# Folded feed-forward units: weight preparation in a written order, modulation dots spread singly

## The chip, the cores and the metric

The kernel runs on one core of a Trainium2 chip. The metric is the device time of one execution in microseconds (us); of several runs the median is taken. Engines are named as in the profile: PE is TensorE (matrix products; PEld are its weight loads), DVE is VectorE, ACT is ScalarE, POOL is GpSimd, SP is SyncE, which issues nearly all DMA transfers.

## The reference

A two-layer model on 256 latent and 256 context tokens of width 1024, in float32. Each layer is a half feed-forward block, a mixer (attention in layer 0, an mLSTM scan in layer 1) and a second half feed-forward block. The change concerns the second feed-forward block of layer 0 and the first of layer 1:

```python
def half_ffn(h, shift, scale, gate, w_in, w_out, g, b):
    xm = modulate(h, shift, scale)              # h * (1 + scale) + shift
    a, u = jnp.split(xm @ w_in, 2, axis=-1)     # 1024 -> 2 x 2816
    y = (jax.nn.silu(a) * u) @ w_out            # 2816 -> 1024
    return post_norm(h, 0.5 * gate * y, g, b)   # layer norm of ALPHA * h + delta
mod_lat = jnp.split((jax.nn.silu(c) @ ada_w[i] + ada_b[i])[:, None, :], N_MOD, axis=-1)
mod_ctx = jnp.split((jax.nn.silu(c_ctx) @ ada_w[i] + ada_b[i])[None, None, :], N_MOD, axis=-1)
```

The shifts, scales and gates are products of a vector with ada_w. They are needed by the blocks that come later.

## The kernel before

**Splitting.** Every float32 operand of a large product is split into a high part, a cast to a reduced format on ScalarE (the copy in split, L212), and a low part, what is left of it, a subtraction on VectorE (L217). A product (mm3) is three matmuls: high by high (L229), high by low (L232), low by high (L233). Activations stand transposed: xh and xl hold 8 blocks d of 128 features by 512 tokens, of which 0 to 255 are latent (LAT) and 256 to 511 context (CTX).

**Weights.** A chunk is 128 x 1024 floats, 512 KB, loaded by raw (L197) from SP's queue into one of 4 buffers and split into one of 7 pairs of buffers (pair, WB = 7). A buffer is used again when its last reader is done.

**A feed-forward block (ffn).** The 22 hidden units of 128 (pairs a and u) are worked in parts. FOLD = {1: ((7, 7, 8), 2), 2: ((6, 8, 8), 1)}: block 1 (second of layer 0) has parts of 7, 7 and 8 units, of which the parts from number 2 on are folded; block 2 (first of layer 1) has 6, 8 and 8, folded from part 1 on. For each part, first unit_in makes g = silu(a) * u for each unit (ffn_g: silu L539 on ScalarE, product L540 on VectorE, split), then unit_out adds the part's share to each of the 8 output blocks d (sum_out, L587 on VectorE). The first 4 units (LEAD) of a block are run on the latent half while the normalization of the context half still goes on, and then on the context half. The last 6 output blocks of the last part (FOLDTAIL) are run by halves, with the next normalization stepped in between (its first product is L398, which needs the sum of L375).

**Folded units** use seven products of quarter size (Strassen's form in Winograd's order) in the place of eight. The inputs' sums are made once, by fold_x (called in the output loop of the part before, at d = 0 and d = 2): sums of high and low (L662), their differences (L666 to L669) and splits, four of them, the last overwriting the context half of xh and xl. The weights' sums are made for each unit by fold_w: two chunks are loaded, r0 is split, half of r1 is split, four sums are made in place (L695 to L698), and r0 and r1 are split once more; that is one cast of 512 columns and three of 1024 on ScalarE, one low part of 512, three of 1024 and four sums on VectorE. In folded, begin(j) calls fold_w(j) and then yields between the seven products (L724); the loop puts the last three products of the unit ahead among the first four of this one. Accumulators are reused: o2 is a copy of o0 after the first product (L735), o0 is copied out to u after the second (L738) and after the fourth (L744), and the sixth product adds to o0 again. VectorE adds to u (L748, L754) and closes the unit (L756).

**Order.** A scheduler in the compiler orders each engine's instructions by program order, by data ready in its own model of time, and by free buffers. Instructions that are passed to pin stay behind the instruction of their engine that stands before them in the program. Before the change, the products of folded units and the dots are pinned; the preparation of weights and the evacuations (L735 to L756) are not.

**Modulation (ada).** A row block of ada_w (512 KB) is loaded by ada_load (L302) into one of two buffers, and ada_dot (L308, on VectorE, pinned) multiplies it with silu(c) or silu(c_ctx) and sums: two dots per row in block 1 (40 rows), one in block 2 (32 rows). FOLDPOP says how many rows are loaded and dotted after which unit or output block: a row's load is issued right ahead of its dots.

## Time and profile before

| | |
|---|---|
| median of 3 runs | 1685.17 us (1683.67 to 1687.54) |
| profiled execution | 1678.48 us, span 1676.4 us |
| granted PE clock over the span | 0.995 |
| busy over the span | PE 97%, PEld 87%, DVE 83%, ACT 43%, POOL 6% |
| block 1 / block 2 of the change, in the span | about 590 to 960 us / 956 to 1330 us |
| the three folded sections (L724) | 819 to 905, 1052 to 1132, 1175 to 1259 us |

Matmuls are pipelined: one that takes 0.28 us in the record starts 0.11 us after the one before it, so loss on PE is read from starts, or from its waits. A row of the waits is "engine, line that waited <- engine, line that ended the wait: us in total, times, longest". A row of the groups is "line, engine, operation, operands, shapes, count | busy us, mean ns of one | idle us of the engine just before them <- what ended it". A row of the timeline is "start us, us, engine, line, operation, shapes, count [idle before <- what ended it]". A row of the windows is "from:to length, PE, PEld, DVE, ACT, POOL busy us (instructions), granted clock, DMA share, GB/s".

### The profile page before, as it was taken

How to read it: one execution, taken by the hardware profiler on the slowest of the kernel's cores; microseconds unless marked ns; L12 is line 12 of the kernel's file. 1: busy time of each engine (PE TensorE's matmuls, PEld its weight loads, DVE VectorE, ACT ScalarE, POOL GpSimd, SP SyncE). 2: the span in 40 equal slices, each digit the busy share in tenths (PEclk: the TensorE clock that was granted, in tenths of full speed). 3: DMA queues.
4: the chain of work that ended last, by engine and by line, in shares of the span. 5: the costliest groups of instructions: out<-in, count | busy, mean ns of one | idle time of the engine just before them, and what ended most of it. 6: DMA issues, size and time to landing. Idle time of an engine off the chain costs nothing. (4 is left out here: it accounts for less than half of the span.)

```text
span 1676.4 us, 26966 instructions
## 1 busy us (share of the span) xinstructions
PE 1617.8 (97%) x10320; PEld 1459.1 (87%) x10320; DVE 1387.7 (83%) x2971; ACT 726.5 (43%) x1286; POOL 93.5 (6%) x114
## 2 busy tenths in 40 slices
PE   7999999999889999999999999999999999999997
PEld 6888888899888897888899998998999888999986
DVE  5799977649988898978987898888888967997686
ACT  4622222314566353223354352552552646566541
POOL 0000000002331100000000100000001002120000
PEclk9999999999999999999999999999999999999999
DMA  9667765522201337765235253346343332337552
GB/s 352 205 216 240 237 212 190 180 69 86 64 1 56 121 108 237 224 198 176 63 101 164 78 195 119 101 152 207 124 160 114 108 126 76 116 124 252 178 176 75
DMA packets 71921, 250.63 MB, mean 150 GB/s; under 512 B 7920, under 2 KB 10480, under 8 KB 71792
## 3 DMA queue, kind: packets, MB, share of 16 engines
q1 hardware_dynamic: 71072, 248.15, 45.7%
q8 instruction: 81, 1.33, 0.3%
q10 hardware_dynamic: 720, 0.76, 0.1%
q14 instruction: 48, 0.39, 0.1%
HBM read 247.83 MB, written 1.05 MB: 148 GB/s over the span
## 5 line engine op out<-in xcount | busy, mean ns | idle before, releaser
L229 PE MATMUL t<-t,t 128*128 128x256 f32 (+2 forms) x2164 | 710.3, 330 | 12.3 <-ACT t L212 9.2
L232 PE MATMUL t<-t,t 128*128 128x256 f32 (+2 forms) x2164 | 710.7, 329 | 2.0 <-DVE t L493 1.1
L233 PE MATMUL t<-t,t 128*128 128x256 f32 (+2 forms) x2164 | 707.5, 328 | 3.1 <-DVE t L217 3.1
L212 ACT CAST t<-t 128x1024 fp32r<-128x1024 f32 (+2 forms) x523 | 442.2, 869 | 498.6 <-PE t L233 189.6
L217 DVE TENSOR_TENSOR t<-t,t 128x256 fp32r<-128x256 f32 (+2 forms) x871 | 547.8, 664 | 99.7 <-ACT t L212 96.5
L229 PEld LDWEIGHTS t<-t,t 128*128 128x128 f32 x2164 | 406.6, 189 | 52.8 <-ACT t L212 11.9
L232 PEld LDWEIGHTS t<-t,t 128*128 128x128 f32 x2164 | 408.7, 189 | 41.0 <-DVE t L493 2.0
L233 PEld LDWEIGHTS t<-t,t 128*128 128x128 f32 x2164 | 407.6, 189 | 41.2 <-DVE t L217 3.7
L308 DVE SCALAR_TENSOR_TENSOR t<-t,t 128x1024 bf16<-128x1024 f32 x224 | 263.2, 1220 | 11.9 <-DMA t<-in_ada_w 11.6
L724 PE MATMUL t<-t,t 128*128 128x256 f32 x2016 | 235.0, 278 | 8.2 <-ACT t L744 3.7
L724 PEld LDWEIGHTS t<-t,t 128*128 128x128 f32 x2016 | 233.1, 188 | 10.6 <-ACT t L744 4.5
L539 ACT ACTIVATE t<-t 128x256 f32<-128x256 f32 (+1 forms) x69 | 33.2, 487 | 131.3 <-PE t L233 130.1
L435 POOL TENSOR_TENSOR t<-t,t 128x256 f32<-128x256 f32 x30 | 23.3, 777 | 1149.4 <-ACT t L425 1147.9
L540 DVE TENSOR_TENSOR t<-t,t 128x256 f32<-128x256 f32 (+1 forms) x69 | 37.4, 549 | 52.9 <-PE t L233 40.3
L587 DVE SCALAR_TENSOR_TENSOR t<-t,t,t 128x256 f32<-128x256 f32 x128 | 57.3, 477 | 28.3 <-PE t L233 28.2
L900 PE MATMUL t<-t,t 128*128 128x256 f32 (+1 forms) x256 | 79.4, 312 | 0.0
L902 PE MATMUL t<-t,t 128*128 128x256 f32 (+1 forms) x256 | 78.8, 310 | 0.0
L901 PE MATMUL t<-t,t 128*128 128x256 f32 (+1 forms) x256 | 78.6, 309 | 0.0
L1339 PE MATMUL t<-t,t 128*128 128x512 f32 (+1 forms) x248 | 55.9, 378 | 10.5 <-ACT t L292 5.0
L1339 PEld LDWEIGHTS t<-t,t 128*128 128x128 f32 x248 | 47.1, 223 | 18.8 <-ACT t L292 5.0
L842 PE MATMUL t<-t,t 128*128 128x512 f32 x264 | 60.0, 389 | 0.0
L425 ACT ACTIVATE t<-t 128x256 f32<-128x256 f32 x72 | 26.1, 413 | 75.1 <-DVE t L418 75.1
(185 smaller groups left out, 1337.6 us busy)
## 6 DMA issues: line engine op xcount, KB each, us to landing
t<-in_ffn_in SPq DMA_DIRECT2D x168, 512.0 KB, 4.3
t<-in_ada_w SPq DMA_DIRECT2D x139, 512.0 KB, 4.0
t<-in_ffn_out SPq DMA_DIRECT2D x66, 512.0 KB, 4.5
t<-in_ffn_last SPq DMA_DIRECT2D x22, 512.0 KB, 3.6
t<-in_att_in SPq DMA_DIRECT2D x12, 512.0 KB, 3.5
t<-in_att_out SPq DMA_DIRECT2D x8, 512.0 KB, 4.0
t<-in_ml_qk SPq DMA_DIRECT2D x8, 512.0 KB, 3.5
t<-in_ml_v SPq DMA_DIRECT2D x8, 512.0 KB, 4.5
```

Source lines behind the costliest of these rows:

```text
L212: self.behind(self.nc.scalar.copy(h, x))
L217: self.behind(self.nc.vector.tensor_tensor(out=ls, in0=xs, in1=hs.bitcast(F32), op=ALU.subtract))
L229: ins = mm(out, wh, xh, start=first, stop=False)
L232: mm(out, wh, xl, start=False, stop=False)
L233: mm(out, wl, xh, start=False, stop=last)
L308: ins = nc.vector.scalar_tensor_tensor(self.tmp().bitcast(BF16), r, 1.0, self.cb[:, v, :], ALU.mult, ALU.mult, accum_out=to)
L724: self.pin(nc.tensor.matmul(o, p, q, start=first and k == i == 0, stop=k == half - 1 and i == 2, skip_group_check=True))
L842: pin(nc.tensor.matmul(ys[tt][i], gs[g], ws[k][w][:, i * 512 : (i + 1) * 512], start=k == 0 and g == w == 0, stop=k == NF - 1 and g == 1,))
L900: mm(o, self.xh[:, k, c], wh, start=k == 0, stop=False)
L901: mm(o, self.xh[:, k, c], wl, start=False, stop=False)
L902: mm(o, self.xl[:, k, c], wh, start=False, stop=k == ND - 1)
L1339: mm = lambda *k, **kw: pin(nc.tensor.matmul(*k, **kw))
```

## The change

- **Weights of folded units.** fold_w no longer loads; fold_load does, two units ahead. The preparation is five steps (first: half split for the last product and two sums; second: split for products one and three; sums: two sums; third and fourth: the two splits of sums). In folded, the steps for unit j + 1 stand between the products of unit j and the last three of unit j - 1, and every instruction there is pinned on its engine, the evacuations too. The order of the products on PE is the one that it was.
- **First folded unit of a section.** Its steps stand before the last output blocks of the part before (load before d = 4, first before 5, second and sums before 6, third and fourth before 7).
- **Output weights after a section.** The first two chunks of w_out are loaded at the last unit but one and split in the last unit's steps.
- **Sums of the inputs.** fold_x stands before the last two unit_in of the part ahead, without the fourth sum; that one, which overwrites xh and xl, is fold_x3 in the output loop at d = 0 and 1 and makes two of its sums again.
- **Modulation.** FOLDPOP gives way to DOTS: (n, points) spreads n calls over points. A unit_in has 4 points (after k = 1, 3, 5, 7), a unit_out 2. A call is one dot; the call of a row's first dot issues the next row's load ahead of it. The first call of a block only loads.

The diff, cut to its core ("unit" in folded is begin without fold_w, with every evacuation pinned and one more yield after the first product):

```diff
-FOLDPOP = {
-    1: {
-        "in": {0: 1, 1: 1, 2: 2, 3: 2, 4: 3, 5: 3, 6: 3} | {j: 2 for j in range(7, 14)},
-        "out": {0: (1, 1, 1, 1, 1, 1, 1, 1), 1: (0, 0, 0, 0, 1, 1, 1, 0)},
-        "tail": {},
-    },
-    2: {
-        "in": {0: 2, 1: 2, 2: 2, 3: 2, 4: 2, 5: 2},
-        "out": {0: (0, 0, 0, 0, 0, 0, 0, 0), 1: (2, 2, 2, 2, 2, 2, 1, 1), 2: (2, 2)},
-        "tail": {(0, 0): 1, (0, 1): 1},
-    },
+DOTS = {
+    1: {"lead": (12, 16), "in0": (14, 12), "out0": (17, 16), "in1": (38, 28)},
+    2: {"lead": (14, 16), "out0": (5, 16), "out1": (14, 12)},
 }
-FOLDX = {0: 0, 2: 1}
...
+        self.raws = {}
+
+    def load(self, c):
+        self.raws[c] = self.b.raw(self.chunks[c])
 
     def __call__(self, i, w=P):
         c, o = divmod(i * P, 1024)
         if c not in self.all:
-            self.all[c] = self.b.chunk(self.chunks[c], self.sh(c))
+            self.all[c] = self.b.chunk(self.chunks[c], self.sh(c), self.raws.get(c))
...
+            seen = {}
+
+            def tick(name):
+                seen[name] = seen.get(name, -1) + 1
+                side.get(("tick", name), lambda m: None)(seen[name])
+
+            def unit_in(j, w, g, steps={}, name=None):
                 n = g[1] - g[0]
                 pa, pu = self.mm(), self.mm()
                 for k in range(ND):
                     for part, o in ((0, pa), (1, pu)):
                         self.mm3(o[:, :n], w(k * 2 + part), self.x(k, g), k == 0, k == ND - 1)
                     self.steps(steps.get((j, k), ""))
+                    if name and k % 2:
+                        tick(name)
                 self.ffn_g(j, pa, pu, g)
 
             def unit_out(hf, d, w, g, steps={}):
                 y = self.mm()
-                part_out(hf, d, w, g, y, range(parts[hf]), steps)
+                n = parts[hf]
+                for js in (range(n // 2), range(n // 2, n)):
+                    part_out(hf, d, w, g, y, js, steps)
+                    if g == allg:
+                        tick(f"out{hf}")
...
+                            unit_in(j, ws[j], g, LEADSTEP if g == LAT else {}, "lead" if g == CTX else None)
+                    for j in first:
                         call("in", j)
                     js = js[LEAD:]
                 folded = None
+                w = (Keep if fold else Stream)(self, [w_out[ends[hf] - parts[hf] + i] for i in range(parts[hf])])
                 if hf >= folds:
                     self.fine = False
-                    folded = self.folded(js, w_in)
+                    folded = self.folded(js, w_in, w, ready)
                     js = []
                 for j in js:
-                    unit_in(j, stream(j), allg)
+                    if fold and hf == folds - 1 and j >= ends[hf] - 2:
+                        self.fold_x(2 * (j + 2 - ends[hf]))
+                    unit_in(j, stream(j), allg, name=f"in{hf}")
...
+                nj = ends[hf]
+                prep = {}
+                if folds <= hf + 1 < len(parts):
+                    self.open = None
+                    rs = []
+                    w22, it = self.fold_w(rs)
+                    go = lambda: next(it)()
+                    prep = {
+                        ND - 4: (lambda: rs.extend(self.fold_load(nj, w_in)),),
+                        ND - 3: (go,),
+                        ND - 2: (go, go),
+                        ND - 1: (go, go),
+                    }
                 for d in range(begun, body):
+                    for f in prep.get(d, ()):
+                        f()
                     unit_out(hf, d, w, allg)
                     call("out", hf, d)
-                    if fold and hf == folds - 1 and d in FOLDX:
-                        self.fold_x(2 * FOLDX[d])
+                    if fold and hf == folds - 1 and d < 2:
+                        self.fold_x3(2 * d)
+                if prep:
+                    ready = w22, self.fold_load(nj + 1, w_in)
                 if body < ND:
                     w = Keep(self, w.chunks, SH, w)
                     self.fine = True
                     for g in groups:
                         for d in range(body, ND):
                             unit_out(hf, d, w, g, tailstep)
-                            call("tail", int(g == CTX), d - body)
...
+    def fold_whole(self, d, g):
+        f = self.tmp().rearrange("p (d f) -> p d f", d=2)
+        h, l = (x[:, d : d + 2, g[0] : g[1]].bitcast(F32) for x in (self.xh, self.xl))
+        self.nc.vector.tensor_tensor(out=f, in0=h, in1=l, op=ALU.add)
+        return f
+
     def fold_x(self, k):
 
-        V, S = self.nc.vector, self.nc.scalar
+        V, S, whole = self.nc.vector, self.nc.scalar, self.fold_whole
         if k == 0:
             self.th, self.tl = (self.t([P, 3, ND // 2, TL], F32R, pool=self.gp) for _ in range(2))
-
-        def whole(d, g):
-            f = self.tmp().rearrange("p (d f) -> p d f", d=2)
-            h, l = (x[:, d : d + 2, g[0] : g[1]].bitcast(F32) for x in (self.xh, self.xl))
-            V.tensor_tensor(out=f, in0=h, in1=l, op=ALU.add)
-            return f
-
-        f11, f12, f21, f22 = whole(k, LAT), whole(k, CTX), whole(ND // 2 + k, LAT), whole(ND // 2 + k, CTX)
-        V.tensor_tensor(out=f11, in0=f11, in1=f12, op=ALU.subtract)
-        V.tensor_tensor(out=f12, in0=f22, in1=f12, op=ALU.subtract)
-        V.tensor_tensor(out=f22, in0=f22, in1=f11, op=ALU.add)
-        V.tensor_tensor(out=f21, in0=f22, in1=f21, op=ALU.subtract)
         ks = slice(k, k + 2)
         to = [[x[:, i, ks, :] for x in (self.th, self.tl)] for i in range(3)]
-        to3 = [x[:, ks, CTX[0] : CTX[1]] for x in (self.xh, self.xl)]
+        f11, f12 = whole(k, LAT), whole(k, CTX)
+        V.tensor_tensor(out=f11, in0=f11, in1=f12, op=ALU.subtract)
         self.split(f11, *to[0])
+        f22 = whole(ND // 2 + k, CTX)
+        V.tensor_tensor(out=f22, in0=f22, in1=f11, op=ALU.add)
         h, l = to[1]
         S.activation(h, f22, AF.Copy, scale=-1.0)
         V.scalar_tensor_tensor(l, f22, -1.0, h.bitcast(F32), ALU.mult, ALU.subtract)
-        self.split(f12, *to3)
+        f21 = whole(ND // 2 + k, LAT)
+        V.tensor_tensor(out=f21, in0=f22, in1=f21, op=ALU.subtract)
         self.split(f21, *to[2])
 
-    def fold_w(self, j, w_in):
-
-        V = self.nc.vector
-        r0, r1 = (self.raw(w_in[2 * j + i]) for i in range(2))
+    def fold_x3(self, k):
+
+        f12, f22 = self.fold_whole(k, CTX), self.fold_whole(ND // 2 + k, CTX)
+        self.nc.vector.tensor_tensor(out=f12, in0=f22, in1=f12, op=ALU.subtract)
+        self.split(f12, *(x[:, k : k + 2, CTX[0] : CTX[1]] for x in (self.xh, self.xl)))
+
+    def fold_load(self, j, w_in):
...
+    def fold_w(self, rs):
+
+        V, S, pin = self.nc.vector, self.nc.scalar, self.pin
         a = slice(0, 512), slice(512, 1024)
-        ps = [self.pair(sh=SH)]
-        self.split(r0, *ps[0])
-        if self.open is None:
-            p, self.open = self.pair(sh=SH), 1
-            self.halves, c = p, a[0]
-        else:
-            p, self.open = self.halves, None
-            c = a[1]
-        w22 = [x[:, c] for x in p]
-        self.split(r1[:, a[0]], *w22)
-        V.tensor_tensor(out=r1[:, a[0]], in0=r1[:, a[0]], in1=r1[:, a[1]], op=ALU.add)
-        V.tensor_tensor(out=r1[:, a[1]], in0=r1[:, a[1]], in1=r0[:, a[0]], op=ALU.add)
-        V.tensor_tensor(out=r0[:, a[0]], in0=r0[:, a[0]], in1=r1[:, a[0]], op=ALU.add)
-        V.tensor_tensor(out=r0[:, a[1]], in0=r0[:, a[1]], in1=r0[:, a[0]], op=ALU.add)
-        for r in (r0, r1):
+        cut = lambda p, i: [x[:, a[i]] for x in p]
+        high = lambda p, r: pin(S.copy(p[0], r))
+        low = lambda p, r: pin(V.tensor_tensor(out=p[1], in0=r, in1=p[0].bitcast(F32), op=ALU.subtract))
+        add = lambda o, p, q: pin(V.tensor_tensor(out=o, in0=p, in1=q, op=ALU.add))
+        w = {}
+
+        def first():
+            r0, r1 = rs
+            if self.open is None:
+                self.open = self.pair(sh=SH)
+                c = 0
+            else:
+                c = 1
+            w["22"] = cut(self.open, c)
+            if c:
+                self.open = None
+            high(w["22"], r1[:, a[0]])
+            low(w["22"], r1[:, a[0]])
+            add(r1[:, a[0]], r1[:, a[0]], r1[:, a[1]])
+            add(r1[:, a[1]], r1[:, a[1]], r0[:, a[0]])
+
+        def second():
+            r0, r1 = rs
             p = self.pair(sh=SH)
-            self.split(r, *p)
-            ps.append(p)
-        cut = lambda p, i: [x[:, a[i]] for x in p]
-        return {"11": cut(ps[0], 0), "12": cut(ps[0], 1), "22": w22,
-                "s2": cut(ps[1], 0), "s4": cut(ps[1], 1), "s1": cut(ps[2], 0), "s3": cut(ps[2], 1)}
-
-    def folded(self, js, w_in):
-
-        nc, V, S = self.nc, self.nc.vector, self.nc.scalar
+            w["11"], w["12"] = cut(p, 0), cut(p, 1)
+            high(p, r0)
+            low(p, r0)
+
+        def sums():
+            r0, r1 = rs
+            add(r0[:, a[0]], r0[:, a[0]], r1[:, a[0]])
+            add(r0[:, a[1]], r0[:, a[1]], r0[:, a[0]])
+
+        def third():
+            r0, r1 = rs
+            p = self.pair(sh=SH)
+            w["s1"], w["s3"] = cut(p, 0), cut(p, 1)
+            high(p, r1)
+            low(p, r1)
+
+        def fourth():
+            r0, r1 = rs
+            p = self.pair(sh=SH)
+            w["s2"], w["s4"] = cut(p, 0), cut(p, 1)
+            high(p, r0)
+            low(p, r0)
+
+        return w, iter((first, second, sums, third, fourth))
...
         before = iter(())
-        for j in js:
-            now = begin(j)
-            next(now)
-            for _ in range(2):
-                next(before, None)
-            for _ in range(2):
-                next(now)
-            next(before, None)
-            next(now)
+        step = lambda g: next(g, None)
+        w, rs = ready
+        nop = lambda: None
+        for i, j in enumerate(js):
+            now = unit(j, w)
+            if i + 1 < len(js):
+                w, prep = self.fold_w(rs)
+            else:
+                prep = iter((nop, lambda: w_out(0), nop, nop, lambda: w_out(len(js))))
+            if i + 2 < len(js):
+                rs = self.fold_load(js[i + 2], w_in)
+            elif i + 2 == len(js):
+                for c in range(2):
+                    w_out.load(c)
+            step(now)
+            next(prep)()
+            step(now)
+            step(before)
+            next(prep)()
+            next(prep)()
+            step(before)
+            next(prep)()
+            step(now)
+            next(prep)()
+            step(now)
+            step(before)
+            step(now)
             before = now
...
+            state = [None, None, 0]
+
+            def dot():
+                cur, nxt, v = state
+                if cur is None:
+                    state[0] = ada[0], b.ada_load(*ada.pop(0)[:2])
+                    return
+                if nxt is None and ada:
+                    state[1] = ada[0], b.ada_load(*ada.pop(0)[:2])
+                (layer, dt, vecs), r = cur
+                b.ada_dot(r, layer, dt, vecs[v])
+                state[2] = v + 1
+                if v + 1 == len(vecs):
+                    state[:] = [state[1], None, 0]
+
+            def tick(m, n, points):
+                for _ in range((m + 1) * n // points - m * n // points):
+                    dot()
+
+            for k, (n, points) in fold.items():
+                s["tick", k] = lambda m, n=n, points=points: tick(m, n, points)
```

50 lines of the change are left out of this document (20 added, 30 removed).

## The prediction

> **What bounds the kernel now.** The page comes first. The profiled execution took 1678.48 us: a span of 1676.4 and 2.1 around it. The median of the three timed runs is 1685.17, 6.7 above; I work the sum against the profiled execution and carry the difference over to the median.
>
> ```profile
> span 1676.4 us, 26966 instructions
> ...
> PE 1617.8 (97%) x10320; PEld 1459.1 (87%) x10320; DVE 1387.7 (83%) x2971; ACT 726.5 (43%) x1286; POOL 93.5 (6%) x114
> ...
> t<-in_ada_w SPq DMA_DIRECT2D x139, 512.0 KB, 4.0
> ```
>
> TensorE is the bound and the change leaves its products and their order alone, so all it can win is idle TensorE time in the two feed-forward blocks that it touches (640 to 1345 us). Hence the next view: TensorE's waits, window by window: 660 to 680; 815 to 905 (first folded section); 1050 to 1130 (second); 1130 to 1180 (start of the third); 1265 to 1345. Columns: total us, times, longest.
>
> ```profile
> PE t L229 <- ACT t L212: 2.2, 1, 2.2
> PE t L232 <- DVE t L217: 0.6, 1, 0.6
> ...
> PE t L724 <- ACT t L212: 2.6, 1, 2.6
> PE t L724 <- ACT t L744: 1.7, 2, 1.5
> PE t L724 <- DVE t L217: 0.8, 1, 0.8
> ...
> PE t L724 <- ACT t L744: 2.0, 2, 1.3
> PE t L724 <- ACT t L735: 0.4, 1, 0.4
> ...
> PE t L724 <- ACT t L735: 0.7, 1, 0.7
> ...
> PE t L398 <- DVE t L375: 1.7, 2, 1.0
> ```
>
> That is the whole purse: some 12 us. Waits that remain elsewhere in these blocks belong to the normalization, which is not changed.
>
> The second loss shows in no wait. Folded matmuls of 256 columns run at two paces; the rows of L724 in 1057 to 1088 us and in 1181 to 1231 us:
>
> ```profile
> L724 PE MATMUL t<-t,t 128*128 128x256 f32 x276 | 31.4, 276 | 0.0
> ...
> L724 PE MATMUL t<-t,t 128*128 128x256 f32 x426 | 50.3, 281 | 0.0
> ```
>
> Taking one duration off the end, (31.4 - 0.28) / 275 is 113 ns from start to start, (50.3 - 0.28) / 425 is 118 ns. A unit has 7 products of 12 matmuls, so 84 take 9.5 us or 9.9 us. The second and third sections both open with a wait for the copy at L735; after it the second runs at 113 ns and later has waits, the third at 118 ns and has none.
>
> **The change, part by part.**
>
> *Dots ahead of the first output product (window 660 to 680).* TensorE first, then DVE:
>
> ```profile
> 667.12 0.39 PE L233 MATMUL t<-t,t 128*128 128x512 f32 x1
> 669.69 0.50 PE L229 MATMUL t<-t,t 128*128 128x512 f32 x1 [2.18 <-ACT t L212]
> 671.11 0.39 PE L233 MATMUL t<-t,t 128*128 128x512 f32 x1
> ...
> 666.01 1.22 DVE L308 SCALAR_TENSOR_TENSOR t<-t,t 128x1024 bf16<-128x1024 f32 x1 [0.98 <-DMA t<-in_ada_w]
> 668.30 0.68 DVE L540 TENSOR_TENSOR t<-t,t 128x512 f32<-128x512 f32 x1
> ```
>
> From 667.12 to 671.11 are 3.99 us for three matmuls that take 0.23 each: 3.3 us lost. The cause is on DVE: the product of the gates (L540) of unit 6 waits behind dots (L308), and one of these waits 0.98 us for its row. The change takes 4 dots out of the stretch before it (18 after units 4 to 6 become 14), spreads them singly and asks for each row a dot earlier. The gates' product may then be up to about 2.6 us late: 18 matmuls (4.1 us) come ahead of the one that needs it, less product and cast. A dot takes 1.15 (from 666.01 to 668.30 are two); four are 4.6 us, more than the 3.3. I take -3.3 (ends: 0 and -3.3).
>
> *Weights of the first folded unit.* They move from the section's start to the output products before it.
>
> ```profile
> 818.92 1.58 PE L724 MATMUL t<-t,t 128*128 128x256 f32 x12
> 823.11 0.50 PE L724 MATMUL t<-t,t 128*128 128x256 f32 x2 [2.61 <-ACT t L212]
> 824.37 0.86 PE L724 MATMUL t<-t,t 128*128 128x256 f32 x5 [0.76 <-DVE t L217]
> ```
>
> From 818.92 to 824.37 are 5.45 us for 14 matmuls worth 1.65: 3.8 lost, waiting for the third and fourth casts of the unit and their low part. What stays is the copy of the first product (L735), which the second product of a first unit has to wait for in every section: 0.7 in the third. So -3.0 (ends: 0 and -3.1). Sections two and three have only that wait at their start: 0.
>
> *The fixed order in the loop.* Same instructions, now pinned on ScalarE and VectorE. What matters is the ring that closes once per unit. Rows of 1181 to 1238 us, VectorE and then ScalarE; then three low parts in a row, and one sum two units apart:
>
> ```profile
> L217 DVE TENSOR_TENSOR t<-t,t 128x1024 fp32r<-128x1024 f32 x16 | 19.3, 1219 | 3.9 <-ACT t L212 3.9
> L217 DVE TENSOR_TENSOR t<-t,t 128x512 fp32r<-128x512 f32 x11 | 7.5, 688 | 2.4 <-ACT t L212 2.4
> L698 DVE TENSOR_TENSOR t<-t 128x512 f32<-128x512 f32 x6 | 4.1, 689 | 0.1
> L756 DVE SCALAR_TENSOR_TENSOR t<-t,t 128x512 f32<-128x512 f32 x5 | 3.4, 689 | 0.7 <-DVE t L754 0.5
> L748 DVE TENSOR_TENSOR t<-t,t 128x256 f32<-128x256 f32 x6 | 2.5, 420 | 1.1 <-PE t L724 1.1
> ...
> L212 ACT CAST t<-t 128x512 fp32r<-128x512 f32 x11 | 6.7, 619 | 7.6 <-DMA t<-in_ffn_in 3.4 <-PE t L724 2.5 <-DVE t L756 1.7
> ...
> 1058.11 3.50 DVE L217 TENSOR_TENSOR t<-t,t 128x1024 fp32r<-128x1024 f32 x3 [1.69 <-ACT t L212]
> ...
> 1196.68 0.69 DVE L697 TENSOR_TENSOR t<-t,t 128x512 f32<-128x512 f32 x1
> 1216.56 0.69 DVE L697 TENSOR_TENSOR t<-t,t 128x512 f32<-128x512 f32 x1
> ```
>
> In the new order VectorE does for one unit: a low part of 512 columns, four sums, three low parts of 1024, two additions of 256 (L748, L754) and the closing product (L756): 0.69 + 4 x 0.69 + 3 x 1.22 + 2 x 0.42 + 0.69 = 8.6 us. From that product to the next low part the ring leads over ScalarE: cast of the gated unit 0.62, copy of u (L744, taken like the addition, 0.4), cast for the next unit 0.62: 1.6. Upper end 10.2 us per unit. Neighbours overlap by 0.08 (three low parts take 3.50, not 3.66), in twelve steps about 0.9: lower end 9.3, where TensorE's own 9.5 holds. Now a unit takes 9.94 (1196.68 to 1216.56 are two), or 9.5 plus the waits. I take 9.85, in the middle, which is 0.07 less; three sections with seven steps from unit to unit make 21: -1.5 us (ends: 21 x -0.44 = -9 and 21 x +0.3 = +6). Behind a late cast ScalarE holds the copy of u, for which the sixth product of the unit waits on TensorE: that is the place where an overlong ring shows (PE <- ACT L744). So I expect little from the pinning itself: stalls of 1.7 and 2.0 become smaller and more even, or the pace goes to 118 ns; either gives 9.85 to 9.9.
>
> [...]
>
> *The dots of the second block's tail* (6, of which 2 are in the tail itself) are done before it. The last, by the row, holds up the sum that the normalization's first product waits for:
>
> ```profile
> 1277.61 1.23 DVE L308 SCALAR_TENSOR_TENSOR t<-t,t 128x1024 bf16<-128x1024 f32 x1 [0.17 <-DMA t<-in_ada_w]
> ```
>
> The wait L398 <- L375 stands twice there. One of its two goes, 1.7 - 1.0: -0.7 (ends 0 and -1.0).
>
> *Where the moved work lands.* VectorE has gaps in only two places, the first two rows below (first block, units 7 to 13; second block, units 4 and 5); the third and fourth are the second block's lead and first output products; ahead of them the low parts of 703 to 780 us:
>
> ```profile
> L217 DVE TENSOR_TENSOR t<-t,t 128x1024 fp32r<-128x1024 f32 x16 | 19.5, 1221 | 2.2 <-ACT t L212 2.2
> ...
> 705.00:780.00 75.00, 75.00 (x333) 62.10 (x332) 58.04 (x94) 21.37 (x26) 0.00 (x0) 1.00 0.64 202
> 1000.00:1022.00 22.00, 22.00 (x99) 18.22 (x98) 14.38 (x34) 6.45 (x8) 0.00 (x0) 1.00 0.73 258
> 978.00:1000.00 22.00, 22.00 (x184) 21.51 (x183) 21.64 (x55) 13.38 (x24) 0.00 (x0) 1.00 0.72 245
> 1022.00:1053.00 31.00, 31.00 (x144) 25.87 (x142) 29.52 (x55) 9.09 (x13) 0.00 (x0) 1.00 0.12 35
> ```
>
> First block: 38 dots instead of 28 (10 x 1.15 = 11.5 us) and both calls of fold_x, 20 operations at 0.61 = 12, go into a stretch with 17 us free. Of the 7 us too many, 2.4 are covered by low parts that can wait (16 are done there, its own units need 14) and 2.6 by the slack at unit 13's end; without this cover they are a stall like the one at 667. Some 2 are left; part of the fold work can also go ahead of unit 7. I take +1 (ends 0 and +7). Second block, 978 to 1053: 9.5 us free; 18 dots instead of 12 (6.9) and 4 more fold operations (2.4; fold_x3 makes two sums again) fill all of it, so the weights of unit 6 may come late: +1 (ends 0 and +4). Weight loads on SP queue behind row loads that wait for one of two row buffers; with two units of raw weights in flight I cost that at 0.
>
> Sum: -3.3 - 3.0 - 1.5 - 0.7 + 1 + 1 = -6.5 us: 1672.0 for a profiled execution, **1678.7** at the median, 0.4% faster.
>
> **Rivals.** (a) *All of it*: the ring closes in TensorE's 9.5, nothing moved is late: -3.3 - 3.0 - 8 - 0.7 = -15, 1670. For it: VectorE idles 6 us for ScalarE in the 57 us of the rows above. Against: the pace of 118 ns comes exactly where nothing waits, and costs 0.4 a unit. [...]
>
> (b) *Gain lost again*: in the second block a row serves one dot. Landing 4.0, dot 1.2, two buffers: one row per 2.6 us; the lead has 14 calls in 22 us, one per 1.6. Pinned dots then hold VectorE 1 us each, 13 us, in a stretch that has 0.4 free; about half is taken by the gaps after it, the rest is a stall before unit 6: +6, 1685, no change. For: VectorE already waits for rows at 666 and 1277. Against: what is not pinned can be placed ahead of a dot.
>
> (c) *Slower*: the ring. If each of the twelve handovers costs 0.08 more where I took an overlap, a unit takes 10.25 to 10.6. At 10.4: 21 x 0.49 = +10 instead of -1.5, total +5: 1690. It decides from about 10.2 us per unit on, where the sections give back the 6 us won elsewhere. For: waits for L744 exist now. Against: the present order reaches 9.94 although VectorE idles those 6 us.
>
> (d) *The order is in effect what it was* (the planner had found the same): the loop changes nothing, only the dots and the first unit do: -5, 1680; it counts with the forecast.
>
> **How the numbers follow.** A difference within 0.2% (3.4 us) can't be told from none with runs that spread as these do. Chances: forecast with (d) 0.52, (a) 0.13, (b) 0.21, (c) 0.14. Faster: most of the forecast (0.50), all of (a), a little of (b): 0.64; same 0.22; slower 0.14. The range runs from (a)'s 1670 to 1688, short of (c); the forecast alone would have 1674 to 1683.
>
> **What would show it.** Right: no wait of TensorE for L212 or L217 before the first folded product of block one, only the copy's 0.4 to 0.7; none before the first output product at 667; units 9.8 to 9.9 apart in all three sections; no dot after the last output product before the second block's tail. Wrong: units more than 10.2 apart with waits for the copy of u; a new wait of TensorE at the end of units 13 or 5, or at unit 6; VectorE idle for in_ada_w in the second block's lead.

## The result and the profile after

The changed kernel is slower: 1695.48 us median of 6 runs (1691.71 to 1697.97) against 1682.82 of the kernel before (1681.00 to 1687.54) on the same chip, ratio 1.0070, 95% interval 1.0052 to 1.0088. The forecast was 1678.7, faster. The profiled execution took 1696.95 us, 18.5 more than the profiled one of before. That is more than the 12.7 of the medians, since that run of before lay 4.3 us under its median and this one 1.5 over its own. I sort the 18.5 by place and use ratios for the sizes. A ratio is that of the mean times, which is why 1.0070 is a little less than the medians give.

From here on lines are those of the changed kernel: the cast of a split is L207, its low part L212, a row load L297, a dot L303, silu L534, the gates' product L535, sum_out L594, the three matmuls L224, L227, L228. In fold_w the casts are L716, low parts L717, sums L718. A folded product is L781; the copy o2 is L790, the first copy of u L793, the second L799, the closing product L811, the cast of the gated unit L812.

The page, the two lines that answer to those of before:

```profile
span 1695.1 us, 26960 instructions
...
PE 1630.0 (96%) x10320; PEld 1466.8 (87%) x10320; DVE 1401.5 (83%) x2979; ACT 725.5 (43%) x1286; POOL 93.9 (6%) x114
```

TensorE has 10320 matmuls as before, in the same order but for 56 places where neighbouring matmuls changed turns, so the start of the matmul with the same number can be compared in both traces. After minus before is -1.7 us as unit 4 of block 1 starts, +2.0 behind the first output product (675) and still when the first section starts, -1.2 behind that section's opening, -0.2 at its end, +5.8 after the first output product of block 2 (1030), +6.1 when the second section starts, +8.9 at its end, +14.7 when the third starts, +15.6 at its end. One gain as expected (3.2 at the first section's opening), three stalls that are new or longer (3.7, 6.0 and 5.8), and 1.0 to 2.8 more within each section. TensorE's waits in those windows (640 to 700; 815 to 908; 1000 to 1057; 1057 to 1146; 1137 to 1190; 1188 to 1277; 1277 to 1360), columns as before:

```profile
PE t L224 <- ACT t L207: 4.8, 1, 4.8
...
PE t L781 <- ACT t L799: 1.3, 1, 1.3
PE t L781 <- ACT t L790: 0.4, 1, 0.4
...
PE t L224 <- ACT t L207: 3.3, 2, 2.5
...
PE t L781 <- ACT t L799: 2.3, 5, 0.9
...
PE t L228 <- DVE t L212: 3.4, 1, 3.4
...
PE t L781 <- ACT t L799: 0.6, 1, 0.6
...
PE t L393 <- DVE t L370: 0.6, 1, 0.6
```

**Before the first output product (block 1, 665).** The waits of 2.2 and 0.6 us became 4.8 and 0.2; with the slower clock behind them (below) the loss of 3.3 became 7.0. TensorE, ScalarE, VectorE, then the queue of SP:

```profile
665.41 0.39 PE L228 MATMUL t<-t,t 128*128 128x512 f32 x1
670.62 0.50 PE L224 MATMUL t<-t,t 128*128 128x512 f32 x1 [4.82 <-ACT t L207]
...
656.65 3.61 ACT L207 CAST t<-t 128x1024 fp32r<-128x1024 f32 x4 [2.56 <-DMA t<-in_ffn_out]
666.10 1.05 ACT L207 CAST t<-t 128x1024 fp32r<-128x1024 f32 x1 [5.84 <-DMA t<-in_ffn_out]
667.05 0.59 ACT L534 ACTIVATE t<-t 128x512 f32<-128x512 f32 x1
...
660.00 1.22 DVE L212 TENSOR_TENSOR t<-t,t 128x1024 fp32r<-128x1024 f32 x1
...
662.65 3.49 DVE L212 TENSOR_TENSOR t<-t,t 128x1024 fp32r<-128x1024 f32 x3
...
667.68 0.69 DVE L535 TENSOR_TENSOR t<-t,t 128x512 f32<-128x512 f32 x1 [0.39 <-ACT t L534]
...
661.30 2.96 SPq L192 DMA_DIRECT2D t<-in_ffn_out  x2
```

The 18 output matmuls that need no unit 6 end with the one at 665.41; unit 6 itself was done 18 x 0.227 = 4.1 us earlier, at about 661.5. Its silu could start then (in a run below, with 6 dots in these units, it starts at 661.53), but in ScalarE's order it stands behind the cast of the fifth chunk of output weights, and that cast idles 5.84 us for its load: silu at 667.05, gates' product at 667.68. The load is late because a raw buffer was: it was issued at 661.30, when the low part of 660.00 had just ended (661.22). The queue of SP between 640 and 672, weight loads and then row loads, says on whom they wait:

```profile
SPq L192 <- DVE t L212: 9.7, 9, 2.3
SPq L297 <- DVE t L303: 9.3, 5, 2.6
```

The raw buffers are given back by low parts, and the low part of 660.00, like the three at 662.65, stood behind dots. The dots that delayed low parts so delayed a load, a cast, a silu and TensorE. The totals of these rows measure nothing: the first is 9.4 us in the kernel before, and 15.2 in the changed kernel with 6 dots (below), which has no stall. What counts is when the one load is issued.

**After the stalls at 665, 1021 and 1178 the granted clock dropped.** Windows of the changed kernel around them, then of the kernel before around its two:

```profile
664.00:671.00 7.00, 2.18 (x9) 1.33 (x8) 5.52 (x8) 3.10 (x4) 0.00 (x0) 1.00 0.95 312
671.00:675.00 4.00, 3.77 (x11) 2.90 (x11) 3.83 (x7) 1.05 (x1) 0.00 (x0) 0.57 0.56 181
...
1026.00:1029.50 3.50, 3.50 (x10) 2.72 (x9) 3.50 (x7) 1.64 (x3) 0.00 (x0) 0.51 0.00 0
...
1183.00:1187.50 4.50, 4.50 (x14) 3.53 (x15) 2.07 (x4) 0.62 (x1) 0.00 (x0) 0.62 0.92 347
```

```profile
671.00:676.00 5.00, 5.00 (x23) 4.11 (x23) 5.00 (x10) 1.06 (x1) 0.00 (x0) 1.00 0.73 222
...
824.40:830.00 5.60, 5.60 (x49) 5.60 (x50) 4.42 (x5) 3.24 (x6) 0.00 (x0) 1.00 0.61 187
```

A clock of 0.57 over 4 us costs 0.43 x 4 = 1.7 us, and the other two come to 1.7 each as well (0.49 x 3.5 and 0.38 x 4.5). Inside these windows the granted clock is 0.50 from 671.0 to 674.4, from 1026.0 to 1029.4 and from 1183.0 to 1186.4: each is 3.4 us at half clock. A fourth such stretch (1329.8 to 1333.2, clock 0.50) lies in the normalization behind block 2, after a wait of only 0.9 us. The profiled run of before has none of the four, although it lost 3.3 and 3.8 us to waits and waits 0.8 at the place of the fourth. But that is one execution against one. Its clock over the span was 0.995; other executions of the kernel before had 0.991 in the mean (on each of five chips), and the six of the changed kernel 0.991, so that either loses some 15 us to the clock, an estimate (0.009 of the time). The clock is 6.8 of the 18.5 us of this pair; the 11.7 that remain are about the 0.70%, or 11.8 us, between the kernels, of which the clock is next to nothing.

**The section's loop.** Copies of u (L799) and what stands ahead of one on ScalarE:

```profile
1096.27 0.36 ACT L799 COPY t<-t 128x256 f32<-128x256 f32 x1
...
1103.30 0.38 ACT L796 ACTIVATE t<-t 128x256 f32<-128x256 f32 x1
1105.80 0.62 ACT L812 CAST t<-t 128x512 fp32r<-128x512 f32 x1 [2.13 <-DVE t L811]
1106.33 0.36 ACT L799 COPY t<-t 128x256 f32<-128x256 f32 x1
...
1116.38 0.36 ACT L799 COPY t<-t 128x256 f32<-128x256 f32 x1
...
1127.44 0.37 ACT L799 COPY t<-t 128x256 f32<-128x256 f32 x1
```

By these copies, units follow each other by 10.06, 10.05 and 11.06 us there. The copy for this unit stands behind the cast of the gated unit *before* it (L812), for which ScalarE idles 2.13 us.

**Before the third section (1178).** ScalarE, then VectorE:

```profile
1176.61 1.05 ACT L716 CAST t<-t 128x1024 fp32r<-128x1024 f32 x1 [4.93 <-DVE t L718]
1177.56 1.04 ACT L207 CAST t<-t 128x1024 fp32r<-128x1024 f32 x1
...
1178.50 0.88 DVE L594 SCALAR_TENSOR_TENSOR t<-t,t,t 128x256 f32<-128x256 f32 x2 [1.98 <-PE t L228]
1179.29 2.35 DVE L717 TENSOR_TENSOR t<-t,t 128x1024 fp32r<-128x1024 f32 x2
1181.56 1.22 DVE L212 TENSOR_TENSOR t<-t,t 128x1024 fp32r<-128x1024 f32 x1
```

The third and fourth steps of the next section's first unit are pinned behind sum_out of output block 6 (L594). The last chunk of output weights, which block 7 needs now, is cast and subtracted behind them: 3.4 us of waiting on TensorE, 5.8 lost in all with the slower clock.

### The profile page after: what moved, and what is told of

It is laid out like the page before. It is cut to its first block, busy times and chain, and to the rows that moved or that the text cites. A ratio compares the mean times of both kernels' runs of the same rounds, so it can differ in the third digit from the quotient of the medians.

```text
span 1695.1 us, 26960 instructions
## 1 busy us (share of the span) xinstructions
PE 1630.0 (96%) x10320; PEld 1466.8 (87%) x10320; DVE 1401.5 (83%) x2979; ACT 725.5 (43%) x1286; POOL 93.9 (6%) x114
## 4 chain that ended last, share of the span: by engine, by line
PE 68%; DVE 21%; ACT 5%; DMA 3%; issue 2%; POOL 0%; ACTq 0%; DVEq 0%; SPq 0%
PE t L224 17%; PE t L228 17%; PE t L227 17%; PE t L916 4%; DVE t L212 3%; DVE t L717 3%; PE t L781 3%; DVE t L718 3%; PE t L1413 2%; ACT t L716 2%; PE t L974 1%; DMA t<-in_ada_w 1%; PE t L975 1%; PE t L976 1%; ACT t L207 1%
## 5 line engine op out<-in xcount | busy, mean ns | idle before, releaser
L224 PE MATMUL t<-t,t 128*128 128x256 f32 (+2 forms) x2164 | 713.5, 332 | 18.5 <-ACT t L207 15.3
L228 PE MATMUL t<-t,t 128*128 128x256 f32 (+2 forms) x2164 | 710.4, 330 | 6.4 <-DVE t L212 6.4
L227 PE MATMUL t<-t,t 128*128 128x256 f32 (+2 forms) x2164 | 714.0, 331 | 2.0 <-DVE t L488 1.1
L207 ACT CAST t<-t 128x1024 fp32r<-128x1024 f32 (+2 forms) x403 | 341.0, 866 | 436.8 <-PE t L228 181.5
L212 DVE TENSOR_TENSOR t<-t,t 128x256 fp32r<-128x256 f32 (+2 forms) x751 | 430.7, 610 | 72.8 <-ACT t L207 71.6
L224 PEld LDWEIGHTS t<-t,t 128*128 128x128 f32 x2164 | 408.8, 190 | 60.4 <-ACT t L207 19.1
L228 PEld LDWEIGHTS t<-t,t 128*128 128x128 f32 x2164 | 409.6, 190 | 46.0 <-DVE t L212 8.0
L227 PEld LDWEIGHTS t<-t,t 128*128 128x128 f32 x2164 | 410.3, 190 | 41.8 <-DVE t L488 2.0
L303 DVE SCALAR_TENSOR_TENSOR t<-t,t 128x1024 bf16<-128x1024 f32 x224 | 265.0, 1221 | 24.7 <-DMA t<-in_ada_w 24.5
L781 PE MATMUL t<-t,t 128*128 128x256 f32 x2016 | 238.2, 279 | 6.5 <-ACT t L799 4.2
L781 PEld LDWEIGHTS t<-t,t 128*128 128x128 f32 x2016 | 235.4, 188 | 9.9 <-ACT t L799 6.1
L716 ACT CAST t<-t 128x512 fp32r<-128x512 f32 (+1 forms) x96 | 90.4, 942 | 87.1 <-DVE t L718 69.7
L717 DVE TENSOR_TENSOR t<-t,t 128x512 fp32r<-128x512 f32 (+1 forms) x96 | 103.8, 1086 | 2.6 <-ACT t L716 0.3
L594 DVE SCALAR_TENSOR_TENSOR t<-t,t,t 128x256 f32<-128x256 f32 x128 | 56.9, 479 | 50.7 <-PE t L228 50.5
L534 ACT ACTIVATE t<-t 128x256 f32<-128x256 f32 (+1 forms) x69 | 33.1, 485 | 107.7 <-PE t L228 105.9
L535 DVE TENSOR_TENSOR t<-t,t 128x256 f32<-128x256 f32 (+1 forms) x69 | 37.5, 549 | 35.4 <-PE t L228 28.2
L1413 PE MATMUL t<-t,t 128*128 128x512 f32 (+1 forms) x248 | 55.6, 377 | 10.2 <-ACT t L287 4.8
```

The source lines that it names most:

```text
L207: self.behind(self.nc.scalar.copy(h, x))
L212: self.behind(self.nc.vector.tensor_tensor(out=ls, in0=xs, in1=hs.bitcast(F32), op=ALU.subtract))
L224: ins = mm(out, wh, xh, start=first, stop=False)
L227: mm(out, wh, xl, start=False, stop=False)
L228: mm(out, wl, xh, start=False, stop=last)
L303: ins = nc.vector.scalar_tensor_tensor(self.tmp().bitcast(BF16), r, 1.0, self.cb[:, v, :], ALU.mult, ALU.mult, accum_out=to)
```

## The experiments

Each time stands with its ratio to the kernel before on the same chip and a 95% interval. The difference of two such ratios is uncertain by some 4 us. A stall is named by its start in us and counts the time by which starts of matmuls are late, the slower clock after it included; it is read from one trace. Diffs are cut to their core.

**The parts by themselves.** *Old dots in the changed kernel.*

```diff
-fold=DOTS[1], fold=DOTS[2]
+fold=FOLDPOP[1], fold=FOLDPOP[2]
```

> The changed kernel with the modulation rows and dots as they were before (FOLDPOP), all else new. Theory A (row loads hold up SP's queue, output weight chunks come late, their casts block ScalarE and with it the silu of the unit before the first output product): the stalls at 665 and 1021 us of the changed kernel (6.9 and 6 us) fall to 3.3 and under 1, the time to about 1687. Theory B (VectorE is full because fold_x stands before the last two units): the stall at 1021 stays, about 1692. The stall of 3.6 us plus half clock at 1179 is not touched by either and stays.

1694.93, 1.0067 (1.0047 to 1.0088): as slow. The stalls at 666 and 1020 shrank to 2.3 and 1.4, but ahead of the third section TensorE lost 11.3 us over the last output chunk. So the loss is not the dots alone. *New dots in the kernel before* (the same edit the other way round):

> The kernel before with the new spreading of rows and dots alone (DOTS). Theory A: it brings the stalls before the first output products by itself (some 4 us more at 667, 6 at 1021), less 0.7 in the tail: about 1691, against 1683 of the kernel before. Theory B: no stall at 1021, the one at 667 gets smaller: 1680 to 1684.

1682.91, 1.0003 (0.9983 to 1.0023): nothing. The first section opens with 0.6 us lost instead of 3.8 although no weight preparation was moved, the tail's stall is gone, and 667 costs 7.1 instead of 3.3. *The fixed loop alone:*

```diff
-                if folds <= hf + 1 < len(parts):
+                if False:
...
-        w, rs = ready
+        rs = self.fold_load(js[0], w_in)
+        w, it = self.fold_w(rs, lambda ins: ins)
```

(with the old dots, fold_x in its old place and no output chunk split early)

> The kernel before with only the folded loop changed: unit's preparation placed in fixed order among the products of the unit ahead. Dots, sums of x, first unit's weights and output chunks as before. Theory (the loop itself is worth nothing here: folded units already follow each other at about 9.9 us, TensorE bound): 1681 to 1685, folded units 9.8 to 10.0 us apart. Rival 1 (my prediction's term for the loop, -1.5 us, or more): 1680 or less. Rival 2 (the fixed order costs a wait per section for the copies that stand behind the preparation's steps): 1686 to 1690, with waits of TensorE for the copies of o2 and of u at over 1 us a section.

1687.49, 1.0031 (1.0008 to 1.0055): the second rival. TensorE waits 4.8, 2.3 and 2.3 us a section for the copies of o2 and of u, and by its copies of u every section ends with a step of 11.1 us. Not all of the time is the loop's: in this trace 667 costs 6.0 instead of 3.3, and up to there nothing was edited.

**What makes the three stalls?** *Rows from POOL's queue,* so that no weight load stands behind a row load:

```diff
-        self.nc.sync.dma_start(r, self.a["ada_w"][layer, dt])
+        (self.nc.gpsimd if layer else self.nc.sync).dma_start(r, self.a["ada_w"][layer, dt])
```

> The changed kernel with the rows of both blocks loaded from POOL's queue in the place of SP's; dots stay where they are. Theory A: chunks no longer queue behind rows that wait for a buffer; the stalls at 665 and 1021 go or shrink below 2 us each, about 1685. Theory B: the stall at 1021 stays, about 1693. If the dots' wait for their rows itself is what holds VectorE, nothing changes at 1021: 1695.

1702.92, 1.0116 (1.0095 to 1.0137): the theory falls. TensorE still waits 4.7 us at 667, and SP's weight loads, now alone in their queue, between 640 and 675:

```profile
SPq L192 <- DVE t L212: 34.3, 10, 9.1
```

They wait for low parts to free raw buffers, and the fifth chunk's load is again issued (664.30) as a low part ends (664.24); the row loads were not what held it. The stall at 1021 became one of 10.5; why is open. *The last output chunk ahead of the third and fourth steps:*

```diff
-                        ND - 1: (go, go),
+                        ND - 1: (lambda: w(ND * parts[hf] - 1), go, go),
```

> The changed kernel, with the output weights' last chunk split ahead of the third and fourth step of the first folded unit (w called for it before them). Theory C (these steps are pinned behind the sums of the output block before, and the chunk for the last output block stands behind them on ScalarE and VectorE): the stall of 3.6 us at 1179 and the half clock behind it (1.8) go, about 1690. Rival: the chunk is late because it was loaded late; then 1695 and the stall stays.

1691.34, 1.0046 (1.0027 to 1.0065): the stall at 1178 is gone, the others stay. *The sums of x back in the output loop:*

```diff
-                    if fold and hf == folds - 1 and j >= ends[hf] - 2:
-                        self.fold_x(2 * (j + 2 - ends[hf]))
...
-                    if fold and hf == folds - 1 and d < 2:
-                        self.fold_x3(2 * d)
+                    if fold and hf == folds - 1 and d in (0, 2):
+                        self.fold_x(d)
+                        self.fold_x3(d)
```

> The changed kernel with one thing undone: the sums of x over pairs of blocks (all of them) are made in the output loop again, where they were before, instead of in the last two whole units. Theory B (the stall at 1021 us of the changed kernel, 5.6 us, comes from these VectorE sums standing ahead of the gates' products of units 4 and 5 in block 2): the stall falls to about the 2 us that dots alone leave there, and the time from 1695.5 to about 1691. Rival (it is the chunk casts and late loads alone; the sums only fill VectorE's idle time): the stall stays at 5 us or more and the time at 1694 to 1697. Second rival (the sums in the output loop hold the next chunks' low parts): new waits for low parts in the output loops after 690 and 1060 us, 1697 or more.

1703.41, 1.0144 (1.0129 to 1.0159): the second rival's time, and in part its place. Waits for low parts of 0.9 and 0.4 us appear at 1056 and 1059, none after 690; but most is elsewhere: the stall at 1021 stays and grows (5.4 and 3.3), and one of 3.4, a wait for the copy o2, appears at 1063. *The first unit's weights at the section's start again* (of the edits of the fixed loop alone only the first two shown):

> The changed kernel with the weights of each section's first folded unit prepared at the section's start again, in no fixed order (loads too); all else as in the change. Theory (the moved preparation is half of the stall at 1021 us and all of the one at 1178 us: the first folded unit's two loads take two of the four raw buffers early and keep them through four steps, so that the output chunks' loads, casts and with them the silu on ScalarE come later; and its third and fourth steps stand ahead of the last output chunk): the stall at 1021 falls from 5.6 to about 2, the one at 1178 from 5.6 to under 1, the one at 665 stays at 7, new waits of up to 3 us at section starts; in all 1686 to 1689. Rival (the dots alone make the stalls): 1694 or more.

1688.02, 1.0033 (1.0019 to 1.0047). The 1178 stall went, as expected; the one at 1021 stayed at 5.7, so the moved preparation is not in it. The sections open with the copy's wait alone, as in the run of the new dots by themselves.

**Dots moved away.** *On the kernel before* (the diff is against the run of the new dots alone):

```diff
-    1: {"lead": (12, 16), "in0": (14, 12), "out0": (17, 16), "in1": (38, 28)},
-    2: {"lead": (14, 16), "out0": (5, 16), "out1": (14, 12)},
+    1: {"lead": (12, 16), "in0": (6, 12), "out0": (16, 16), "in1": (40, 28), "out1": (7, 16)},
+    2: {"lead": (9, 16), "in0": (5, 8), "out0": (5, 16), "out1": (14, 12)},
```

> The kernel before with the dots spread singly, as in the run of the new dots alone, but with fewer of them in the last whole units ahead of the output loops (block 1: 6 instead of 14 in units 4 to 6, the rest in the output loops and the later units; block 2: 9 instead of 14 in the lead, 5 in units 4 and 5). Theory (low parts of the output chunks stand behind dots on VectorE, raw buffers come free late, the fifth chunk's load and cast are late, and the silu behind that cast on ScalarE's strict order is late): the 7 us stall at 667 falls to 2 us or less, the 2 us one at 1024 does not grow, time 1674 to 1678. Rival (the stall is set by the chunks' loads and casts themselves, whatever the dots): the stall stays at 5 to 7 us, time 1681 to 1684.

1675.96, 0.9966 (0.9954 to 0.9978). Eight dots fewer in units 4 to 6, and the 7 us are gone. They are gone in all seven runs with 6 dots there. *On the changed kernel:*

> The changed kernel with fewer dots in the last whole units ahead of the output loops, and nothing else. Theory: the stalls at 665 (7.1 us) and 1021 (5.6 us) go, the one at 1178 stays, the pinned loop's small waits stay: 1695.5 - 7 - 5 = 1683 to 1685. Rival (the stall at 1021 is that of the moved preparation and the early sums, whatever the dots): the one at 665 alone goes, 1688 to 1690.

1686.45, 1.0026 (1.0008 to 1.0045): 665 went, 1021 only fell to 4.5. *With sums back and chunk first as well:*

> The changed kernel with three edits: the sums of x back in the output loop, the last output chunk split ahead of the third and fourth steps of the next unit's preparation, and fewer dots in the last whole units ahead of the output loops (as in the other run of that kind). If the three stalls (667, 1021, 1178 us) are all that separates the change from a gain, and each goes as its own run says: 1695.5 - 4 (chunk) - 4 (sums) - 5 (dots) = 1682, or below that where the slower clock after each long stall goes with them (1678 to 1680). Rival (the pinned preparation costs elsewhere, in copies of u at the end of each section and at section starts): 1685 to 1690, with stalls left at 820, 888, 1127 and 1191.

1683.06, 1.0008 (0.9995 to 1.0021): no stall at 665 or 1021 and 2.4 at 1176, and still no gain. Against the same dots on the kernel before, 7 us stay that the three stalls don't explain; the three sections together take 260.4 us against 254.0. *Seven dots moved on* (the diff is against the run just named, on the kernel before):

```diff
-    2: {"lead": (9, 16), "in0": (5, 8), "out0": (5, 16), "out1": (14, 12)},
+    2: {"lead": (9, 16), "in0": (5, 8), "out0": (12, 16), "out1": (7, 12)},
```

> The kernel before with dots spread singly and fewer of them in the last whole units (as in the run that beat both kernels, 0.9966 of the time before), and in the second block seven dots moved on from the second output loop to the first. Theory (a dot that waits 1.4 us for its row holds the copies at the second section's end, a stall of 1.6 us at 1136): that stall goes, 1674 to 1676. Rival (the first output loop of that block is full on VectorE, 29.5 of 31 us: low parts come late there and at the next section's start): 1677 to 1681.

1688.10, 1.0040 (1.0025 to 1.0055): worse than the rival had it: the second section waits 12.6 us for one cast. TensorE between 1046 and 1140, SP between 1020 and 1064 (L294 is the row load there, L300 the dot):

```profile
PE t L725 <- ACT t L204: 12.6, 1, 12.6
...
SPq L294 <- DVE t L300: 30.4, 11, 8.9
```

Row loads that wait for a row buffer hold SP for 30 of 44 us; that this is why the first folded unit's weights came late is likely, not shown.

**The order.** *ScalarE and VectorE free in the folded units:*

```diff
-        V, S, pin = self.nc.vector, self.nc.scalar, self.pin
+        V, S, pin = self.nc.vector, self.nc.scalar, lambda ins: ins
...
-            pin(S.copy(o2, o0))
+            S.copy(o2, o0)
```

(and so on for every copy, silu, addition, closing product and cast of unit)

> The changed kernel with the fixed order taken back on ScalarE and VectorE in the folded units (preparation and copies are placed by the planner; the products of TensorE keep their order; program order, loads and dots as in the change). Theory (the fixed order costs 1 to 2.5 us a section and makes the last output chunk of the section before wait behind the third and fourth steps, 5.6 us at 1178; the stalls at 665 and 1021 are not its doing): 1695.5 - 5 - 4 = 1685 to 1688. Rival 1 (order in effect what it was; only where the loads and dots stand matters): 1693 to 1697. Rival 2 (without the order the planner lets the preparation run late): waits at section starts, above 1697.

1682.50, 1.0003 (0.9992 to 1.0014). Nothing but the pins was taken away, and the whole loss went, with the stalls at 666 and 1017 still there at 4.9 and 6.0 us; the one at 1178 gave way to one of 4.4 at 1141. From start to start, units are 9.52 us apart in all three sections (one at 9.74 and the first of each aside). *Only the preparation pinned:*

> The changed kernel with the fixed order kept for the preparation of weights alone; the copies, silus, additions and casts that follow the products are placed by the planner. Theory (what costs is that a copy that TensorE waits for stands behind a cast of the preparation on ScalarE's strict order; with the copies free the planner puts them ahead): the wait for the copy of u at each section's end goes, units 9.5 to 9.7 us apart, the stall at 1178 (the third and fourth steps ahead of the last output chunk) stays: 1686 to 1689. Rival (the pinned preparation itself keeps the ring long): units at 9.9 to 10.1 in the second half of a section, 1692 to 1696.

1686.89, 1.0024 (1.0012 to 1.0036): 9.52 us a unit, and the stall at 1171 stays. *Only the copies and what closes a unit pinned:*

> The changed kernel with the fixed order kept for the copies, silus, additions and casts behind the products alone; the preparation of weights is placed by the planner. Theory (order between preparation and copies is what costs, and with the preparation free it goes around the copies): units 9.5 to 9.7 us apart, no stall at 1178: 1683 to 1686. Rival (the order among the copies themselves, across two units that overlap, makes the wait for the copy of u): a wait of 1 us or more at each section's end stays, units over 9.9, 1688 to 1692.

1701.04, 1.0106 (1.0091 to 1.0121): units 9.5 to 12.2 us apart. The order among the copies of two overlapping units is what costs; the preparation's costs only ahead of the last output chunk. *One pair exchanged, all of it pinned:* the closing of a unit behind the next unit's copy of u.

```diff
+            yield
             gh, gl = self.gt[j] = tuple(self.t([P, self.gw], F32R, tag=k, bufs=self.gn, pool=self.gp) for k in ("gh", "gl"))
             pin(V.scalar_tensor_tensor(sl, u, -1.0, sl, ALU.mult, ALU.mult))
...
             step(before)
             step(now)
+            step(before)
             before = now
```

> The changed kernel with one edit to the written order, everything still pinned: the closing of a folded unit (its last product on VectorE, the cast of the gated unit on ScalarE, its low part) stands behind the next unit's copy of u instead of ahead of it. Theory (that one pair is what the fixed order loses in the sections: TensorE waits for the copy of u, which waits on ScalarE for the cast of the gated unit of the unit before): units 9.5 us apart throughout, no wait for the copy of u at the sections' ends, sections 82 to 83 us long instead of 85 to 87; the stalls at 665, 1021 and 1178 stay: 1686 to 1688. Rival (another pair of the order closes the ring as soon as this one is open): units still 9.8 us or more, 1692 or more.

1686.73, 1.0032 (1.0019 to 1.0045). ScalarE in this kernel (L800 is the copy of u, L814 the cast of the gated unit):

```profile
1089.78 0.38 ACT L800 COPY t<-t 128x256 f32<-128x256 f32 x1 [0.50 <-PE t L782]
...
1098.78 0.37 ACT L797 ACTIVATE t<-t 128x256 f32<-128x256 f32 x1
1099.30 0.38 ACT L800 COPY t<-t 128x256 f32<-128x256 f32 x1
1101.28 0.62 ACT L814 CAST t<-t 128x512 fp32r<-128x512 f32 x1 [1.60 <-DVE t L813]
...
1108.91 0.37 ACT L800 COPY t<-t 128x256 f32<-128x256 f32 x1
```

The copy comes right behind the silu, the idle time for the closing product stands behind it, and the copies are 9.52 and 9.61 us apart. The time from the first folded product of a section to its last:

| us | first | second | third |
|---|---|---|---|
| before | 87.25 | 84.33 | 84.22 |
| changed | 85.07 | 87.17 | 85.19 |
| changed, one pair exchanged | 82.46 | 84.15 | 82.71 |
| changed, ScalarE and VectorE free | 81.75 | 83.00 | 81.75 |

**What it is worth mended.** *One pair exchanged, chunk first, dots moved:*

> The same edit, and the last output chunk split ahead of the third and fourth steps, and fewer dots in the last whole units ahead of the output loops. Theory (these three places are all that keeps the change from a gain): 1695.5 - 8 - 4 - 9 = 1670 to 1674, with a fixed order as fast as the planner's own (1669.6). Rival (the planner's free order gains elsewhere too): 1676 to 1680.

1674.72, 0.9955 (0.9942 to 0.9968). That can't be told from the moved dots on the kernel before (0.9966, 0.9954 to 0.9978). *Free order, dots moved:*

> The changed kernel without the fixed order on ScalarE and VectorE in folded units (as in the run that came out equal to the kernel before) and with fewer dots in the last whole units ahead of the output loops. Theory (the two losses are separate: the fixed order costs about 11 us in the sections and at their ends, the place of the dots 5 us at 665 and 6 to 7 at 1021; the rest of the change, loads two units ahead and steps in program order, is a gain of 2 to 4 us a section): 1682.5 - 5 - 6 = 1671 to 1673, units 9.5 us apart, below both kernels and below the run of the moved dots on the kernel before (1676). Rival (the stall at 1021 belongs to the moved preparation and stays): 1677 to 1679.

1669.61, **0.9928** (0.9916 to 0.9941), faster than both kernels, faster than the moved dots on the kernel before, and by 4.5 us (0.0027) faster than the mended written order. *The same with the sums back:*

> The fastest version so far (no fixed order on ScalarE and VectorE, fewer dots in the last whole units, 0.9928 of the time before) with the sums of x back in the output loop. Theory (with few dots there, the early sums are what still makes the stall of 4.4 us at 1014 to 1020: it went in the run that had both undone): the stall goes, 1665 to 1667. Rival (the sums in the output loop then hold the chunks' low parts and the next section's start, as they did in the run with them alone put back): waits of 2 to 4 us at 1040 to 1060, 1669 to 1674.

1669.69, 0.9935 (0.9919 to 0.9951): the stall at 1014 fell from 4.4 to 0.7 as the theory had it, but the time did not follow, and the rival's waits at 1040 to 1060 are not there either. The two runs can't be told apart.

## Why the prediction was wrong

By ratios to the kernel before, of which 1% is 16.8 us: the change costs +11.8. Exchanging one pair of the order takes 6.4 off (1.0070 to 1.0032; in the traces the three sections are 8.1 shorter), the chunk first 4.0, the dots moved 7.4, each give or take some 4, and all three together 19.3 (to 0.9955). Mended in three places the change is 7.6 us faster than the kernel before, but fewer dots alone give the kernel before 5.7, and the remaining 1.9 is within the intervals. With a free order 6.4 remain, which is not. By the steps of the forecast:

- **Dots before the first output product, -3.3: wrong, +3.7** in the pair of traces (from -1.7 to +2.0). I read the stall off VectorE, as the gates' product behind dots, and counted dots taken out, 18 to 14. After the change that product waits for silu, and silu for a late chunk's cast. The chain through the raw buffers is shown by the times of the one load and by the runs with 6 dots, which have no stall; dots ahead of the *low parts* were the quantity to count. My reading rested on no row of ScalarE. The size is loose: nine runs with 14 dots have the same instructions in the same order on every engine up to there and lose 2.8 to 7.5 us (mean 6.0), three with the old dots 2.4 to 6.0 (mean 3.9). What differs within each group is the execution, not the program up to there.
- **First folded unit, -3.0: right in size (3.2), wrong in cause and price.** New dots alone bring the same 0.6 at that place, since no dot is left in that output loop; old dots with moved preparation bring 0.6 and then 1.6. Either would have done. The price that I put at 0 for the other sections was 5.8 us ahead of the third (3.4 of waiting and 1.7 of clock in it): the pinned steps stood behind sum_out, for which VectorE idled 1.98 us, and with 2.35 us ahead of that chunk's low part at 1181.56. The question "what is queued behind it" was not asked for the last output chunk.
- **Fixed order, -1.5 (-9 to +6): wrong in sign, inside the ends.** The seven steps of each of three sections, taken from the start of a section's second product on, sum to 208.5 us before and 211.2 after, +2.7. I had the ring of VectorE (8.6) plus 1.6 over ScalarE. The rows show that VectorE was not the ring: with one pair exchanged the same pinned work runs at 9.5, TensorE's own pace. The ring was a copy behind the cast of the unit before. I did name the copy of u as the place where it would show, and it did; but the rival put the point where it decides at 10.2 us a unit, and 10.05 for some units with 11 (by the copies) for the last was enough, since the gains that it was to be set against were not there. ScalarE idles 2.13 us ahead of L812 (1105.80), and the copy L799 comes behind it (1106.33): of these 2.13 us TensorE waits 0.25 (to 1106.74) for the copy, and the unit is 0.5 longer.
- **Tail, -0.7: right.** The wait for the sum fell from 1.7 to 0.6.
- **Moved work, +1 in block 1: nothing seen; +1 (0 to +4) in block 2: +6.0,** from -0.2 to +5.8. That is rival (b) at its place and in its size, but not only by its mechanism. VectorE idles for rows in that stretch, as it said, and is not full, as I had assumed:

```profile
1012.17 1.22 DVE L303 SCALAR_TENSOR_TENSOR t<-t,t 128x1024 bf16<-128x1024 f32 x1 [1.47 <-DMA t<-in_ada_w]
1014.62 1.22 DVE L303 SCALAR_TENSOR_TENSOR t<-t,t 128x1024 bf16<-128x1024 f32 x1 [1.21 <-DMA t<-in_ada_w]
...
1015.93 1.35 ACT L207 CAST t<-t 128x1024 fp32r<-128x1024 f32 x2 [8.99 <-DMA t<-in_ffn_out]
1017.71 0.59 ACT L534 ACTIVATE t<-t 128x512 f32<-128x512 f32 x1
...
1021.86 0.68 DVE L535 TENSOR_TENSOR t<-t,t 128x512 f32<-128x512 f32 x1
```

  ScalarE idles 9 us for a chunk again, silu comes after it, and then six operations of the early sums, 3.6 us, stand between silu and unit 4's gates' product at 1021.86. Dots alone give 2.1 there, early sums with old dots 1.4, both 6.0. With either one mended alone 3.7 us or more were left (four runs); with few dots and the sums in their old place under 1 us (four runs). Why the sums alone, taken back, made it longer (8.7) is open.
- **Weight loads behind row loads, 0: right** at the stall at 665, where rows in another queue change nothing; elsewhere in this change it is not shown. The load there was late for want of a raw buffer, which I had not priced.
- **The clock, not priced:** four more stretches at half clock (0.50 granted, 3.4 us each), 6.8 us, in the profiled pair, but the same 0.991 in the mean of either kernel's runs: between the kernels this term is next to nothing.

The slower case had 0.14, all on the ring. Its upper end for a unit, 10.6, follows from no sum: twelve handovers of 0.08 on 9.3 are 10.26. What was missed is that three places could fail at once and each by more than its bound, because I bounded each by VectorE's free time, while the delay ran over ScalarE's order and the raw buffers. Rival (a), 9.5 us a unit, is there as soon as the order is free; which of the other parts (loads two units ahead, steps in program order) gives it is not shown.

Open: what sets the stall before the first output product within its spread of 2.8 to 7.5 us when the instructions are the same. The 6.0 with the fixed loop alone is such a case: up to there, that run has the instructions of the kernel before in the same order.

## What to carry to other kernels

Before work is moved ahead of a deadline, follow the buffer that it delays to its next load and to what stands behind that load: here ScalarE idled 5.84 us for one, with silu next in its order, and the free time that I had counted on VectorE did not show it. In a written order for two overlapping units, no instruction that TensorE waits for may stand behind one that waits for the end of the unit before: exchanging one such pair took 6.4 us off here. Try an order without its pins first: here the planner's own order of the same program ran at 9.52 us a unit, where 84 matmuls at 113 ns are 9.5.
